# Loads of split weights written down one half tile sooner

## The chip, the core and the metric

The kernel runs on one core of a Trainium2 chip. The metric is the time of one execution on the device, in microseconds (us); smaller is better. The core has a matrix engine (TensorE, PE), three engines for elementwise work (VectorE, DVE; ScalarE, ACT; GpSimd, POOL) and SyncE (SP), whose queue starts all transfers here.

## What is computed

One layer of a hybrid decoder over 512 tokens of width 2048, in float32. The core of the reference:

```python
h = _rms(x, norm_g[l])
proj = h @ w_in[l]                              # 2048 -> 7296
pa, pb, pc = _split(proj, (A_COLS, B_COLS, C_COLS))
...
ya = _rwkv7(r, k, v, wd, ad, ...) * silu(ga)    # 12 heads of 64, a recurrence over the tokens
yb = _pool(pu, pool_w[l], pool_scale[l]) * silu(pg)
yc = _stick_breaking(qc, kc, vc, ...) * silu(gc)  # 12 heads of 64, causal
y = jnp.concatenate([ya, yb, yc], axis=-1) @ w_out[l]
x = x + y
```

## The kernel before

**Weights.** The projections are done with float32 accuracy from three products of a faster format: a weight w is split into wh (w in that format) and wl = w - wh, the input into hh and hl, and each block of 128 x 128 takes three matmuls of 512 columns, hh with wh, hl with wh, hh with wl (`three`). The unit of the stream of weights is a half tile, 128 x 1024 numbers, 512 KB: 108 of w_in (two for each tile of 128 columns of the projection behind the first three) and 32 of w_out. For each one, SP loads `raw` (2 buffers), ACT casts it to `wh` (3 buffers), DVE subtracts to `wl` (2 buffers), and PE runs 24 projection matmuls from the pair. `weights(i)` hands out half tile i and sees to it that i + 1 is written down, at high priority. In this text half tiles are counted from 1 in their order in the stream.

**The chains.** Between the projection matmuls the kernel strews the work of the three branches: six pairs of rwkv heads, six pairs of attention heads, four pooling groups. In the rwkv chain `qm`, `gm`, `gh`, `s`, `y`, `mu`, `var`, `q` and `am` are matmuls; `amr`, `bk`, `bx`, `uv`, `yc` are their operands on DVE, and `pr` and `xblk` are a long row of small DVE operations that eliminate a block of 32. In attention `z` are the scores, `n` and `w` the scans and exponentials, `wT` the transposes, `wt` their copies by ACT, `o` the products. `u` empties the projection's PSUM bank (`pj`, 2 banks).

**What sets the order.** Each branch is a generator. After every projection matmul `pump()` asks a planner, `Pace`, whether the next step of a branch may be written down: Pace keeps a clock of its own, adds up costs of matmuls, books the elementwise work of each engine (`record`) and each transfer (`transfer`, with a landing DL later by its reckoning), and a step is written down when the planner thinks that its operands are ready. The program's order so found, with the priorities of `tc.high_priority`, is the order in which every engine runs its instructions; no engine looks ahead at run time. So what the planner is told of a transfer moves the steps of the branches on all engines:

```python
def transfer(self, out, src):
    at = max(self.now, self.ready.get(self.key(src), 0.0))
    if at < self.now + 1.0:
        at = self.queue = max(at, self.queue) + 0.45
    self.ready[self.key(out)] = at + DL
```

Of the kernel before, what the change touches and what calls it, by code (L numbers as in the profile page):

```python
# [8 lines left out]
F32 = mybir.dt.float32  # L9
# [4 lines left out]
P = 128  # L14
# [41 lines left out]
AHEAD = 300  # L56
# [161 lines left out]
def hybrid_trunk_kernel(ctx: ExitStack, tc: tile.TileContext, x, xT, w_in, w_out, vecs, consts, up_w, pool_w, out):  # L218
# [5 lines left out]
    def dma(out, in_, queue=nc.sync):  # L224
        pace.transfer(out, in_)
        queue.dma_start(out=out, in_=in_)
# [3 lines left out]
    wp = ctx.enter_context(tc.tile_pool(name="wp", bufs=2))  # L230
# [9 lines left out]
    def name(s):  # L240
        uid[0] += 1
        return f"{s}_{uid[0]}"
# [199 lines left out]

    HK = KT // 2

    def split_weights(src):
        raw = wp.tile([P, HK * P], F32, tag="raw", bufs=2, name=name("raw"))
        dma(out=raw, in_=src)
        wh = wp.tile([P, HK * P], F32R, tag="wh", bufs=3, name=name("wh"))
        wl = wp.tile([P, HK * P], F32R, tag="wl", name=name("wl"))
        act.copy(out=wh, in_=raw)  # L450
        dve.tensor_tensor(wl, raw, wh.bitcast(F32), ALU.subtract)
        return wh, wl
# [9 lines left out]
    stream = []  # L462
# [7 lines left out]
    fetched = {}  # L470

    def fetch(i):
        if i < len(stream) and i not in fetched:
            with tc.high_priority(offset=AHEAD if i > 1 else 60):
                fetched[i] = split_weights(stream[i])

    def weights(i):
        fetch(i)
        fetch(i + 1)
        return fetched.pop(i)  # L480

    def project(n):
        o = pj()
        for half in range(2):
            wh, wl = weights(2 * (n - NFIRST) + half)
            for j in range(HK):
                k = half * HK + j
                sl = slice(j * P, (j + 1) * P)
                three(o, wh[:, sl], wl[:, sl], hh[k], hl[k], k == 0, k == KT - 1)
        return o  # L490
# [509 lines left out]
    for kq in range(KT // KQ):  # L1000
        parts = []
        for j in range(KQ):
            load_h(kq * KQ + j)
            if j < NFIRST:
                raw = raw0[kq, j]
# [65 lines left out]
    for nb in range(4):  # L1071
        accs = []
        for tb in range(4):
            accs.append(bank(tags[used % 8], "oacc"))
            used += 1
        for i2 in range(KT // 2):
            if nb == 0:
                split_y(2 * i2)
                split_y(2 * i2 + 1)
            wh, wl = weights(first_out + nb * (KT // 2) + i2)  # L1080
            for tb in range(4):
                ts_ = slice(tb * P, (tb + 1) * P)
                for i in (2 * i2, 2 * i2 + 1):
                    k = Y_ORDER[i]
                    sl = slice((i % 2) * 512, (i % 2) * 512 + 512)
                    three(accs[tb], yh[k][:, ts_], yl[k][:, ts_], wh[:, sl], wl[:, sl], i == 0, i == KT - 1)
        for tb in range(4):
            xr = tmp("xr")
            dma(out=xr, in_=x[tb * P:(tb + 1) * P, nb * 512:(nb + 1) * 512])
            dve.tensor_tensor(xr, accs[tb], xr, ALU.add)  # L1090
            dma(out=out[tb * P:(tb + 1) * P, nb * 512:(nb + 1) * 512], in_=xr)
# [72 lines left out]
```

## Time and profile before

| what | value |
|---|---|
| median of 3 runs | 1008.57 us (1006.39 to 1008.71) |
| the profiled execution | 1007.96 us, of which the span in the trace is 1006.1 us |
| PE busy | 978.3 us, 97% of the span |
| DVE, ACT, POOL busy | 662.2, 511.6, 140.5 us (66%, 51%, 14%) |
| mean granted clock of PE | 0.996 |
| a load of a half tile | 512 KB, 3.4 us from issue to landing |
| cast wh, subtraction wl | 1046 ns and 1246 ns, 140 of each |

A share of busy time is a mean over the span. PE's matmuls are pipelined: what counts is the distance from the start of one to the start of the next.

### The profile page before, as it was taken

To read this page: it belongs to the slowest core of one execution; us is meant where nothing else is said; L and a number is where in the kernel's file an instruction comes from. 1 tells how busy PE (TensorE), PEld (TensorE's weight loads), DVE (VectorE), ACT (ScalarE), POOL (GpSimd) and SP (SyncE) were. 2 spreads that over 40 slices of the span, in tenths; PEclk is the share of its full clock that TensorE was granted. 3 is DMA by queue.
4 is the path that set the end of the run, shared out by engine and by line. 5 is a ranking of instruction groups with operands and counts; after the bars stand their busy time and mean duration, and the time that the engine had idled before them with its cause. 6 is when DMAs were issued, how large, how long until landed. Compare 5 with 4: busy or idle time off the path is not lost. (4 is left out here: it accounts for less than half of the span.)

```text
span 1006.1 us, 13872 instructions
## 1 busy us (share of the span) xinstructions
PE 978.3 (97%) x5132; PEld 786.9 (78%) x5132; DVE 662.2 (66%) x1249; ACT 511.6 (51%) x838; POOL 140.5 (14%) x204
## 2 busy tenths in 40 slices
PE   8999999999899998999999999999999999999998
PEld 7867876888678886788768887788867888888886
DVE  5369784888849885697947979398864666323232
ACT  5656654756556654647546565466552245221210
POOL 0131211121120302112111111203211010000000
PEclk9999999999999999999999999999999999999999
DMA  9622322132321313223131222313232248624241
GB/s 337 216 90 76 103 85 90 63 111 68 105 84 58 114 65 106 79 84 95 64 121 64 90 89 80 105 63 110 72 106 79 98 145 281 219 87 147 93 138 63
DMA packets 62210, 109.17 MB, mean 109 GB/s; under 512 B 29760, under 2 KB 31168, under 8 KB 62144
## 3 DMA queue, kind: packets, MB, share of 16 engines
q1 hardware_dynamic: 62144, 108.30, 32.1%
q8 instruction: 40, 0.66, 0.3%
q14 instruction: 26, 0.21, 0.1%
HBM read 98.84 MB, written 9.44 MB: 108 GB/s over the span
## 5 line engine op out<-in xcount | busy, mean ns | idle before, releaser
L380 PE MATMUL pj<-hh,wl 128*128 128x512 f32 x864 | 343.7, 398 | 7.8 <-DVE wl L212 7.5
L380 PE MATMUL pj<-hh,wh 128*128 128x512 f32 x864 | 345.8, 400 | 0.1
L380 PE MATMUL pj<-hl,wh 128*128 128x512 f32 x864 | 343.4, 398 | 0.0
L212 DVE TENSOR_TENSOR wl<-raw,wh 128x1024 fp32r<-128x1024 f32 x140 | 174.4, 1246 | 174.6 <-PE oacc L380 86.1
L212 ACT CAST wh<-raw 128x1024 fp32r<-128x1024 f32 x140 | 146.4, 1046 | 205.7 <-PE oacc L380 95.2
L380 PEld LDWEIGHTS pj<-hh,wl 128*128 128x128 f32 x864 | 162.8, 188 | 45.7 <-DVE wl L212 12.4
L380 PEld LDWEIGHTS pj<-hh,wh 128*128 128x128 f32 x864 | 162.8, 188 | 33.6 <-issue 1.8
L380 PEld LDWEIGHTS pj<-hl,wh 128*128 128x128 f32 x864 | 163.0, 189 | 32.6 <-issue 2.2
L380 PE MATMUL oacc<-wl,yh 128*128 128x512 f32 x256 | 100.1, 391 | 0.0
L380 PE MATMUL oacc<-wh,yh 128*128 128x512 f32 x256 | 99.8, 390 | 0.0
L380 PE MATMUL oacc<-wh,yl 128*128 128x512 f32 x256 | 99.7, 390 | 0.0
L212 POOL TENSOR_SCALAR e<-e 128x512 f32<-128x512 f32 x28 | 45.2, 1614 | 197.4 <-ACT e L212 179.4
L380 PEld LDWEIGHTS oacc<-wh,yl 128*128 128x128 f32 x256 | 48.1, 188 | 10.3 <-issue 0.2
L380 PEld LDWEIGHTS oacc<-wl,yh 128*128 128x128 f32 x256 | 48.1, 188 | 10.2 <-issue 0.2
L380 PEld LDWEIGHTS oacc<-wh,yh 128*128 128x128 f32 x256 | 48.1, 188 | 10.0 <-DVE u L212 0.2
L212 POOL TENSOR_TENSOR d<-u 128x512 f32<-128x512 f32 x25 | 29.4, 1176 | 149.3 <-DVE xblk L212 67.6
L212 DVE TENSOR_TENSOR pr<-xblk,nblk 128x60 f32<-128x60 f32 (+8 forms) x180 | 46.5, 258 | 5.0
L212 ACT ACTIVATE e<-e 128x512 f32<-128x512 f32 x50 | 31.5, 630 | 35.7 <-POOL e L212 35.3
L212 DVE TENSOR_TENSOR_SCAN n<-n,m 128x512 f32<-128x512 f32 (+3 forms) x48 | 43.8, 923 | 7.5 <-ACT n L212 7.5
L212 DVE TENSOR_TENSOR xblk<-xblk,pr 128x60 f32<-128x60 f32 (+8 forms) x180 | 39.3, 218 | 5.0
L212 POOL CAST kl<-klo 64x512 fp32r<-64x512 f32 x24 | 19.2, 802 | 150.4 <-DVE klo L212 134.9
L212 ACT ACTIVATE n<-n 128x512 f32<-128x512 f32 (+1 forms) x72 | 39.6, 551 | 0.4
(203 smaller groups left out, 1227.5 us busy)
## 6 DMA issues: line engine op xcount, KB each, us to landing
raw<-in_w_in SPq DMA_DIRECT2D x108, 512.0 KB, 3.4
raw<-in_w_out SPq DMA_DIRECT2D x32, 512.0 KB, 3.4
lt<-in_x SPq DMA_DIRECT2D x8, 512.0 KB
xr<-in_x SPq DMA_DIRECT2D x16, 256.0 KB, 5.5
out<-xr SPq DMA_DIRECT2D x16, 256.0 KB, 4.1
yin<-yd SPq DMA_DIRECT2D x14, 256.0 KB, 4.6
fr<-in_w_in SPq DMA_DIRECT2D x12, 256.0 KB, 6.9
nblk<-s SPq DMA_DIRECT2D x24, 128.0 KB, 3.4
```

The lines of the kernel that those rows point to most:

```text
L212: return call(*args, **kw)
L380: pe.matmul(o, lhsT, rhs, start=start, stop=stop)
```

## The change

The load is taken out of `split_weights` into `load_weights`, and `weights(i)`, besides writing down half tile i + 1, writes down the load of half tile i + 2. The number of buffers of `raw` stays 2, and no other line changes.

```diff
--- before.py
+++ after.py
@@ -442,9 +442,16 @@
 
     HK = KT // 2
 
-    def split_weights(src):
-        raw = wp.tile([P, HK * P], F32, tag="raw", bufs=2, name=name("raw"))
-        dma(out=raw, in_=src)
+    raws = {}
+
+    def load_weights(i):
+        if i < len(stream) and i not in raws and i not in fetched:
+            raws[i] = wp.tile([P, HK * P], F32, tag="raw", bufs=2, name=name("raw"))
+            dma(out=raws[i], in_=stream[i])
+
+    def split_weights(i):
+        load_weights(i)
+        raw = raws.pop(i)
         wh = wp.tile([P, HK * P], F32R, tag="wh", bufs=3, name=name("wh"))
         wl = wp.tile([P, HK * P], F32R, tag="wl", name=name("wl"))
         act.copy(out=wh, in_=raw)
@@ -472,11 +479,13 @@
     def fetch(i):
         if i < len(stream) and i not in fetched:
             with tc.high_priority(offset=AHEAD if i > 1 else 60):
-                fetched[i] = split_weights(stream[i])
+                fetched[i] = split_weights(i)
 
     def weights(i):
         fetch(i)
         fetch(i + 1)
+        with tc.high_priority(offset=AHEAD):
+            load_weights(i + 2)
         return fetched.pop(i)
 
     def project(n):
```

Every engine has the same instructions in both kernels; their order differs. The order at two places, the first and the fourth pair of heads:

**First pair, DVE.** From the emptying of a bank by u to the emptying of the next. `u_670<-pj_561` and `u_688<-pj_563` are the same step. Before:

```order
L212 TENSOR_TENSOR u_670<-pj_561,rstd 128x512
L212 TENSOR_TENSOR wl_729<-raw_726,wh_728 128x1024
L212 TENSOR_TENSOR amr<-sq_500,E_644 64x8x64
L212 TENSOR_TENSOR c_642<-sq_500,e_619 128x512
L212 SCALAR_TENSOR_TENSOR u_559<-u_559,nvec,y_87_661 128x512
L212 SCALAR_TENSOR_TENSOR bk_693<-c_642,e_611 64x8x64
L212 SCALAR_TENSOR_TENSOR qs_570<-qm_658,qs_570 128x512
L212 TENSOR_TENSOR sl_684<-qs_681,sh_683 128x512
L212 TENSOR_TENSOR e_619<-e_619,d_485 128x512
L212 TENSOR_TENSOR wl_762<-raw_759,wh_761 128x1024
L212 TENSOR_TENSOR cq_569<-u_559,qs_570 128x512
L212 TENSOR_TENSOR bk_693<-e_619,e_611 64x8x64
```

(amr<-d,E and m stand four and five rows below the last one shown, and the next u<-pj behind m.) After:

```order
L212 TENSOR_TENSOR cq_571<-u_561,qs_572 128x512
L212 TENSOR_TENSOR wl_762<-raw_732,wh_761 128x1024
L212 TENSOR_TENSOR bk_676<-e_621,e_613 64x8x64
L212 SCALAR_TENSOR_TENSOR bk_676<-c_639,e_613 64x8x64
L212 TENSOR_TENSOR bk_676<-e_621,e_613 64x8x64
L212 TENSOR_TENSOR amr<-sq_502,E_641 64x8x64
L212 TENSOR_TENSOR amr<-d_493,E_641 128x8x64
L212 SCALAR_TENSOR_TENSOR m_90_684<-d_493,vec,e_621 128x512
L212 TENSOR_TENSOR u_688<-pj_563,rstd 128x512
L212 TENSOR_TENSOR q_124_879<-cq_571,q_124_879 64x512
L212 TENSOR_TENSOR sl_702<-qs_699,sh_701 128x512
L212 TENSOR_TENSOR u_758<-pj_690,rstd 128x512
```

The step u<-pj stood ahead of the split, and now stands behind amr<-d and m; sl has moved behind it.

**First pair, PE.** The end of one projection tile and the start of the next, at the same matmul in both. Before:

```order
L380 MATMUL pj_672<-hl_131,wh_675 128x512
L380 MATMUL pj_672<-hh_115,wl_676 128x512
L380 MATMUL pj_758<-hh_100,wh_728 128x512
L380 MATMUL pj_758<-hl_116,wh_728 128x512
L380 MATMUL pj_758<-hh_100,wl_729 128x512
L380 MATMUL pj_758<-hh_101,wh_728 128x512
L380 MATMUL qm_769<-sh_683,bmean_r 128x512
L380 MATMUL qm_769<-sl_684,bmean_r 128x512
L380 MATMUL pj_758<-hl_117,wh_728 128x512
```

After:

```order
L380 MATMUL pj_690<-hl_131,wh_691 128x512
L380 MATMUL pj_690<-hh_115,wl_692 128x512
L380 MATMUL gm_776<-amr,bk_676 128x128
L380 MATMUL gm_777<-amr,bk_676 128x128
L380 MATMUL gm_776<-amr,bk_676 128x128
L380 MATMUL pj_760<-hh_100,wh_728 128x512
L380 MATMUL pj_760<-hl_116,wh_728 128x512
L380 MATMUL pj_760<-hh_100,wl_729 128x512
L380 MATMUL pj_760<-hh_101,wh_728 128x512
```

The matmuls gm, which before stood 25 rows behind the first row shown here of tile pj_758, stand ahead of the tile now; qm stands 26 rows further down.

**Fourth pair, DVE.** The 64th and the 65th split (wl_4665 and wl_4713 before, wl_4683 and wl_4735 after) and what lies between them. Before:

```order
L212 TENSOR_TENSOR wl_4665<-raw_4662,wh_4664 128x1024
L212 TENSOR_TENSOR u_4655<-pj_4527,rstd 128x512
L212 TENSOR_TENSOR pr_4439<-xblk_4390,nblk_4389 128x28
L212 TENSOR_TENSOR xblk_4390<-xblk_4390,pr_4439 128x7x4
L212 TENSOR_TENSOR pr_4439<-xblk_4390,nblk_4389 128x21
L212 TENSOR_TENSOR xblk_4390<-xblk_4390,pr_4439 128x7x3
L212 SCALAR_TENSOR_TENSOR d_4658<-d_4658,vec,u_4655 128x512
L212 SCALAR_TENSOR_TENSOR yc_4074<-yc_4074,vec,sq_4515 128x512
L212 SCALAR_TENSOR_TENSOR n_4619<-n_4619,m_4620 128x384
L212 SCALAR_TENSOR_TENSOR yc_4074<-yc_4074,vec,bv_2960 128x512
L212 SCALAR_TENSOR_TENSOR n_4619<-n_4619,m_4620 128x128
L212 TENSOR_TENSOR y_3636<-yc_4074,y_3636 128x512
```

The next row is the 65th split. After:

```order
L212 SCALAR_TENSOR_TENSOR yc_4034<-yc_4034,vec,bv_2921 128x512
L212 TENSOR_TENSOR y_3645<-yc_4034,y_3645 128x512
L212 SCALAR_TENSOR_TENSOR n_4652<-n_4652,m_4653 128x256
L212 TENSOR_TENSOR wl_4683<-raw_4631,wh_4682 128x1024
L212 TENSOR_TENSOR u_4675<-pj_4555,rstd 128x512
L212 TENSOR_TENSOR w_4647<-w_4647,n_4652 128x256
L212 SCALAR_TENSOR_TENSOR d_4678<-d_4678,vec,u_4675 128x512
L212 TENSOR_TENSOR bv_4046<-bv_4046,d_4678 128x512
L212 TENSOR_TENSOR wl_4735<-raw_4686,wh_4734 128x1024
L212 TENSOR_TENSOR wl_4786<-raw_4738,wh_4785 128x1024
```

Of the rows that lay between the two splits, pr, xblk, yc, n and y stand ahead of the 64th now; u, d and bv are left, and a w that stood behind the 65th.

**Fourth pair, ACT.** The casts of half tiles and the copies wt (wh_4888 before and wh_4908 after are the 68th half tile's). Before:

```order
L212 CAST wh_4825<-raw_4823 128x1024
L212 COPY wt_4795<-wT_4790 128x512
L212 ACTIVATE e_4769<-d_4766 128x512
L212 ACTIVATE e_4769<-e_4769 128x512 x2
L212 CAST wh_4888<-raw_4886 128x1024
L212 COPY wt_4821<-wT_4816 128x512
L212 COPY wt_4836<-wT_4831 128x512
L212 COPY wt_4870<-wT_4867 128x256
```

After:

```order
L212 CAST wh_4855<-raw_4789 128x1024
L212 COPY wt_4802<-wT_4797 128x512
L212 ACTIVATE e_4778<-d_4775 128x512
L212 COPY wt_4811<-wT_4806 128x512
L212 ACTIVATE e_4778<-e_4778 128x512 x2
L212 CAST sh_4879<-up_4877 128x256
L212 ACTIVATE sq_4883<-d_4418,vec 128x512
L212 CAST sh_4885<-sq_4883 128x512
L212 COPY wt_4845<-wT_4842 128x256
L212 CAST wh_4908<-raw_4859 128x1024
```

The two copies wt_4821 and wt_4836 stood behind the cast of the 68th half tile; the same two, wt_4802 and wt_4811, stand ahead of it now.

## Rows read from the trace of the kernel before

**Rows 1.** The page, section 1: busy time (share of the span) and instructions of each engine.
```profile
PE 978.3 (97%) x5132; PEld 786.9 (78%) x5132; DVE 662.2 (66%) x1249; ACT 511.6 (51%) x838; POOL 140.5 (14%) x204
```

**Rows 2.** Waits of PE: who waited for whom, us in total, times, longest.
```profile
PE pj L380 <- DVE wl L212: 7.5, 8, 1.8
PE o L380 <- ACT wt L212: 4.4, 4, 1.7
PE wT L384 <- ACT w L212: 3.4, 4, 0.9
```

**Rows 3.** Timeline of PE, fourth pair: start us, us, engine, line, operation [idle before <-releaser].
```profile
470.75 0.38 PE L380 MATMUL y<-bx,uv 128*128 128x128 f32 x2
...
496.24 0.39 PE L380 MATMUL pj<-hl,wh 128*128 128x512 f32 x1
496.77 0.50 PE L380 MATMUL pj<-hh,wl 128*128 128x512 f32 x1
...
502.60 0.39 PE L380 MATMUL pj<-hl,wh 128*128 128x512 f32 x1
503.80 0.51 PE L380 MATMUL pj<-hh,wl 128*128 128x512 f32 x1 [0.80 <-DVE wl L212]
```

**Rows 4.** Windows of PE: us, PE busy (matmuls), granted clock, DMA share, GB/s.
```profile
735.30:738.70 3.40, 3.40 (x12) 0.50 0.35 135
160.00:163.50 3.50, 3.05 (x15) 1.00 0.00 0
```

**Rows 5.** Waits of SP's queue, and section 6 of the page: KB each, us to landing.
```profile
SPq L226 <- DVE wl L212: 636.4, 123, 10.7
...
raw<-in_w_in SPq DMA_DIRECT2D x108, 512.0 KB, 3.4
```

**Rows 6.** Timeline of DVE, fourth pair, with the 64th and the 65th split.
```profile
475.34 0.69 DVE L212 TENSOR_TENSOR sl<-yc,sh 128x512 fp32r<-128x512 f32 x1 [2.07 <-ACT sh L212]
...
495.50 1.22 DVE L212 TENSOR_TENSOR wl<-raw,wh 128x1024 fp32r<-128x1024 f32 x1
...
500.10 0.94 DVE L212 TENSOR_TENSOR_SCAN n<-n,m 128x384 f32<-128x384 f32 x1
...
501.61 0.41 DVE L212 TENSOR_TENSOR_SCAN n<-n,m 128x128 f32<-128x128 f32 x1
...
502.53 1.21 DVE L212 TENSOR_TENSOR wl<-raw,wh 128x1024 fp32r<-128x1024 f32 x1
```

**Rows 7.** Timeline of SP, fourth pair: loads issued.
```profile
503.81 0.33 SPq L226 DMA_DIRECT2D raw<-in_w_in  x1
...
512.02 0.39 SPq L226 DMA_DIRECT2D raw<-in_w_in  x1
```

**Rows 8.** Timeline of DVE, first pair.
```profile
78.00 0.67 DVE L212 TENSOR_TENSOR u<-pj,rstd 128x512 f32<-128x512 f32 x1
...
82.79 0.67 DVE L212 TENSOR_TENSOR sl<-qs,sh 128x512 fp32r<-128x512 f32 x1
83.39 0.67 DVE L212 TENSOR_TENSOR e<-e,d 128x512 f32<-128x512 f32 x1
...
88.94 0.75 DVE L212 SCALAR_TENSOR_TENSOR m<-d,vec,e 128x512 f32<-128x512 f32 x1
89.60 0.68 DVE L212 TENSOR_TENSOR u<-pj,rstd 128x512 f32<-128x512 f32 x1
```

**Rows 9.** Timeline of PE, first pair.
```profile
81.46 0.39 PE L380 MATMUL pj<-hh,wh 128*128 128x512 f32 x1
...
83.52 0.51 PE L380 MATMUL qm<-sl,bmean_r 128*128 128x512 f32 x1 [0.75 <-DVE sl L212]
...
89.08 1.16 PE L380 MATMUL gm<-amr,bk 64*128 64x128 f32 x16 [0.74 <-DVE amr L212]
```

**Rows 10.** Timeline of ACT, fourth pair.
```profile
473.21 1.05 ACT L212 CAST wh<-raw 128x1024 fp32r<-128x1024 f32 x1
...
515.84 1.05 ACT L212 CAST wh<-raw 128x1024 fp32r<-128x1024 f32 x1 [1.16 <-DMA raw<-in_w_in]
```

## The prediction

> **What bounds the kernel now.** I read the page first: TensorE (PE) is busy for 978.3 of 1006.1 us, VectorE (DVE) for two thirds [rows 1]. The number of matmuls doesn't change, so the change can only give or take what PE loses between them. Next I read PE's waits. From 100 us on three kinds of wait make up nearly all of its idle time: projections that wait for wl, the low half of a split weight, 7.5 us in 8 waits; attention's o that waits for the copied wt, 4.4 in 4; the transpose wT that waits for the exponential w, 3.4 in 4 [rows 2]. A wait costs some 0.16 us more than its idle time: between the starts 502.60 and 503.80 lie 1.20 us where 0.23 is usual, so 0.97 is lost with 0.80 idle [rows 3]. All of it is then 15.3 + 16 x 0.16 = 17.9 us, and some smaller waits add about 1.8 (three for wl of 0.3 each, as behind 496.24, one for s, one for mu): 19.7. The last wait for wl, 1.8 us at 732, was followed by 3.4 us at a granted clock of 0.50, its lower level of 1.2 GHz [rows 4], which cost 1.7, nearly as much again as the wait. So about **21 us** are there to be had.
>
> Why is wl late? Not because its load is. A load is 512 KB and lands after 3.4 us; the queue of loads (SP) spent 636.4 us in 123 waits for a wl [rows 5]. That is the raw buffer: there are two, and a load may only start when the split two half tiles back has read its buffer. The wl at 502.53 ends at 503.74 [rows 6], and SP issues a load at 503.81 [rows 7]. **So a load can't go a half tile sooner**: written down earlier, it waits for the same wl. The Trainium skill ("DMA: Bandwidth & Descriptors", anatomy of one DMA) says that a DMA's semaphore wait is held by the issuing sequencer, before dispatch; SP's row agrees. By that rule an early load only blocks SP's queue sooner, which speaks against the change; the third rival prices that from rows.
>
> wl is late since DVE is full. From sl at 475.34 to the split of the 64th half tile at 495.50 + 1.22 DVE has no gap of note: 21.4 us of elimination (pr, xblk), scans and splits, and PE wants that split at 496.47; the 65th, at 502.53, stands behind 5.8 us more [rows 3, 6].
>
> **The change, part by part.** The same instructions, transfers and buffers are there before and after. The raw tile is allocated a half tile sooner and the load placed on SP one to three rows earlier: nothing, as above, while a wl frees the buffer. What does change is Pace's clock: it books the load earlier, thinks wh and wl done earlier, and so places the chain steps (rwkv, attention) 20 to 40 projections sooner between the projections. The sum comes from these moves, at 0.2275 us a projection.
>
> *First pair, a loss.* In the order of before, PE had 44 projections, then qm, and gm 23 projections behind the place where gm stands now. gm needs amr, the product with E, and DVE's rows up to it are nearly the same in both. Up to 78.00 DVE has the same rows. Then u and sl have gone behind, 0.6 each by the step from 82.79 to 83.39, so amr, which ended when m began, 88.94 [rows 8], is read by gm from 89.08 on [rows 9] and now from 89.08 - 1.2 = 87.9; with ACT's squares a little later, up to 88.2. PE reaches gm at 81.46 [rows 9]. Worse, the projection behind gm needs the PSUM bank that u empties, and u now stands behind m: m begins at 88.94 - 1.2 = 87.7, and with 0.66 for m and 0.68 for u that gives 89.1, or 89.4 with ACT's delay. PE can do three gm meanwhile (0.4). It loses 89.1 - 81.46 - 0.4 = 7.2 us, or 7.5, where before qm and gm cost 0.75 and 0.74 idle [rows 9], 1.8 in all. **+5.6.** After such a gap I expect the half clock of 732 once: **+1.7**. The bounds are 0 (a gap of 1.7 us at 158 was followed by 3.5 us at full clock [rows 4]) and twice that; I take the value of the row with the longer idle stretch. The Trainium skill ("TensorE: Matmul & The Clock Gate", Part 1) has TensorE fall to its lower level after idling and climb back with work. By it this gap would surely end in half clock, as I took; without any fall the sum would be 1.7 lower.
>
> *First pair, a gain.* PE comes 5.6 us late to this pair's waits, two for wl and the longest for wt, 1.7 idle [rows 2], which are shorter than that: 3.8 of the 21 us may go.
>
> *Second pair.* The steps move by unequal amounts here. The second block of gm stands too close behind the rows that fill its operands; with DVE's pitches it waits about 1.3 us, the two gh 0.2 and 0.4, less 0.4 that goes: **+1.5**. Its two waits for wl and the one for w, 3.1 of the 21, go by the reckoning of the next part.
>
> *The steady pairs.* Take the 64th split. y, the matmul at 470.75 from which sl is made, moves 39 projections up, 8.9 us. Before, PE started it 25.7 us ahead of its need of the 64th wl; now 25.7 + 8.9 + 1.3 (two pairs of z and four transposes that come between) = 35.9 us. DVE: sl began 4.6 us after y, for ScalarE (ACT) had the cast of wh at 473.21, 1.05 us, between the two copies of yc [rows 10]. Now both copies stand together with one exponential behind: 2.4 us. Then come the 21.4 us, and 11.1 us more that used to lie outside: two splits (1.14 each), u, q and d (0.6 to 0.7 each), scans of 384 and 128 and two of 256 (0.87, 0.34, 0.60), two multiplications by w (0.94), two yc and y (1.9), and the last rows of pr and xblk (1.7). The end is at 2.4 + 21.4 + 11.1 = 34.9, **1.0 us before** the need, where it was 0.25 after. If sl takes 4.6 again, it is 1.2 late. The work between the 64th and 65th split falls from 5.8 us to 2.1 (u, w, d, bv), and PE has 24 projections, 5.5 us, between them: the wait for the 65th goes even if the 64th is late. The exponential w, which followed that split, comes with it, and wT has 31 projections, not 26, between its first two groups: those waits go too.
>
> *o.* ACT's copies of wt stood behind the cast of the 68th half tile, which began only at 515.84 [rows 10], since its load was issued only at 512.02 [rows 7], behind a transfer of lt. Now both wt stand ahead of that cast: the wait goes.
>
> Behind the second pair the gain is at most 14.2: what is left of the 21, the wait at 732 with its clock (3.6) among it. Nearer neighbours on the chain (s, gh, am) will bring small waits; I allow 0.3 a pair, **+1.5**, and count only 85% of the gains (3.8 + 3.1 + 14.2 = 21.1) since each slack is about 1 us and the reckoning no better: **-17.9**.
>
> **Sum**: 5.6 + 1.7 + 1.5 + 1.5 - 17.9 = -7.6. The profiled execution took 1007.96 us, 0.6 below the median of 1008.57, so 1000.4 beside this execution and **1001** beside the median.
>
> **Rivals.**
> 1. *Slower: DVE's full stretch stays late.* Its rows stand in a fixed order, and one late operand stops all behind it, splits too; the row of before that stood idle was sl, 2.07 us [rows 6]. If sl takes 4.6 us again and another row in the stretch waits 2.07, the 64th split is 2.2 + 2.07 - 1.0 = 3.3 us late in each of five pairs, 16 us: 1017. It decides from 1.5 us a pair, where the time is 1008.6 again. For it: the stretch is longer and gapless. Against: its operands come from steps that move up with it.
> 2. *Nothing.* The loads are held by the buffers, and what the pairs gain the first pair's hole eats: with sl 4.6 us after y, each pair loses 1.2, 6 us: 1007. For it: the first pair is nearly sure to lose, and each gain rests on about 1 us.
> 3. *SP's queue.* A load that stands sooner before the transfers of s, nblk or lt blocks them for a wait on wl, 636.4/123 = 5.2 us on the mean [rows 5]. If one of them in a pair comes that late, and 3 of the 5.2 us lie beside other work, each of five pairs loses 2: 1011. Against: in the steady order one load instead of two now stands between the first s and xblk.
> 4. *Better.* No fall of the clock, all waits gone, no small ones: 1007.96 + 5.6 + 1.5 - 21.1 = 994.
>
> **How the numbers follow.** This kernel's runs lie 2.3 us apart, so 0.3%, 3 us, is about what can be told from nothing. My forecast (995 to 1005): 0.57. Better (below 995): 0.10. Nothing (1005.5 to 1011.6): 0.16. Slower by rivals 1 and 3: 0.13 and 0.04. That gives faster 0.67, same 0.16, slower 0.17. The range, 992 to 1012, leaves out the far ends of rivals 1 and 4; the forecast's own is 995 to 1005.
>
> **What would show it.** Right: SP still waits some 600 us for wl; an idle stretch of PE from 81.5 to about 89, released by amr and then by u, with half clock behind it; no wait for wt or wT; waits for wl below 0.5 us a pair; a gm of 1 us in the second pair. Wrong: loads that SP issues away from a wl's end; a first pair whose gm meets its amr in time; five equal waits for wl of over 1 us.

## The result, and the profile after

The changed kernel takes **1018.5 us** (median of 4 runs, 1017.1 to 1019.35), the kernel before 1008.64 (4 runs); the ratio is 1.0091, with a 95% interval of 1.0066 to 1.0117. It is slower by 9 to 10 us, where I had forecast 1001. Two single executions beside the experiments, one of the kernel before at 2738.9 us and one of the kernel before with three `wl` buffers at 1072.0, were far slower than all others of their kernel and stand outside the ranges and ratios given.

The page of the profiled execution after, its first line and the busy times (us, share of the span, instructions):

```profile
span 1016.6 us, 13841 instructions
...
PE 980.3 (96%) x5132; PEld 788.4 (78%) x5132; DVE 665.6 (65%) x1249; ACT 510.3 (50%) x838; POOL 135.2 (13%) x204
```

PE is busy for 2.0 us more than before [rows 1], VectorE for 3.4 more, the others for less. So of the 10.5 us more of span 8.5 are idle time of PE. Waits of PE after (who waited for whom, us in total, times, longest):

```profile
PE pj L380 <- DVE wl L212: 11.2, 11, 2.7
PE gm L380 <- issue: 6.7, 1, 6.7
PE s L380 <- DVE bx L212: 3.8, 4, 0.9
...
PE s L380 <- DVE uv L212: 2.0, 4, 0.5
...
PE gm L380 <- DVE bx L212: 0.9, 2, 0.8
...
PE wT L384 <- issue: 0.6, 1, 0.6
PE wT L384 <- ACT w L212: 0.6, 1, 0.6
```

Beside [rows 2] the reader sees four things. The waits for wl have grown, from 7.5 us in 8 to 11.2 in 11. The waits of o for wt (4.4) are gone, those of wT are down from 3.4 to 1.2. Two kinds are new: one gap of 6.7 us ahead of gm, which the view can't put down to an engine ("issue"; the rows below show what ended it), and 5.8 us of s waiting for bx and uv in eight waits. By idle time alone that is 3.7 (wl) + 5.5 (s) + 7.1 (gm) - 4.4 (o) - 2.2 (wT) - 1.1 (qm and mu, which no longer wait), 8.6 us more than before.

The gap stands where the prediction put it. PE, first pair (start us, us, operation, [idle before]), and DVE there:

```profile
80.95 0.39 PE L380 MATMUL pj<-hh,wl 128*128 128x512 f32 x1
88.03 1.19 PE L380 MATMUL gm<-amr,bk 64*128 64x128 f32 x6 [6.70 <-issue]
89.25 0.80 PE L380 MATMUL pj<-hh,wh 128*128 128x512 f32 x1
```

```profile
87.24 0.69 DVE L212 TENSOR_TENSOR amr<-d,E 128x512 f32<-128x512 f32 x1
87.85 0.75 DVE L212 SCALAR_TENSOR_TENSOR m<-d,vec,e 128x512 f32<-128x512 f32 x1
88.51 0.68 DVE L212 TENSOR_TENSOR u<-pj,rstd 128x512 f32<-128x512 f32 x1
```

gm starts when amr<-d,E is written (87.24 + 0.69 = 87.93), the projection behind it when u has emptied its bank (88.51 + 0.68 = 89.19). What came behind, in windows of PE (us, PE busy, granted clock, DMA share, GB/s):

```profile
88.00:92.00 4.00, 3.94 (x13) 0.50 0.02 4
92.00:95.40 3.40, 3.40 (x20) 0.86 0.00 0
```

PE runs at half clock for 4 us and a part of the next 3.4 (a mean of 0.86 is 28% of it at 0.50): 4.9 us in all, which cost about 2.5.

A steady pair, the fourth, beside [rows 3, 6]. PE: the y that sl is made from, and two splits waited for, the 63rd and the 64th:

```profile
471.08 0.38 PE L380 MATMUL y<-bx,uv 128*128 128x128 f32 x2
...
502.09 0.50 PE L380 MATMUL pj<-hh,wl 128*128 128x512 f32 x1 [0.98 <-DVE wl L212]
...
509.06 0.50 PE L380 MATMUL pj<-hh,wl 128*128 128x512 f32 x1 [0.80 <-DVE wl L212]
```

DVE in the same stretch:

```profile
472.67 0.69 DVE L212 TENSOR_TENSOR w<-w,n 128x512 f32<-128x512 f32 x1
...
474.57 0.69 DVE L212 TENSOR_TENSOR sl<-yc,sh 128x512 fp32r<-128x512 f32 x1 [1.20 <-ACT sh L212]
...
475.85 0.52 DVE L212 TENSOR_TENSOR xblk<-xblk,pr 128x29 f32<-128x29 f32 x1
476.40 0.62 DVE L212 TENSOR_TENSOR pr<-xblk,nblk 128x28 f32<-128x28 f32 x1
...
481.30 0.94 DVE L212 TENSOR_TENSOR pr<-xblk,nblk 128x48 f32<-128x48 f32 x1
...
494.84 1.10 DVE L212 TENSOR_TENSOR xblk<-xblk,pr 128x54 f32<-128x54 f32 x1
...
496.25 0.74 DVE L212 SCALAR_TENSOR_TENSOR d<-d,vec,u 128x512 f32<-128x512 f32 x1
...
503.27 1.38 DVE L212 TENSOR_TENSOR_SCAN n<-n,m 128x384 f32<-128x384 f32 x2 [0.15 <-ACT n L212]
...
507.80 1.20 DVE L212 TENSOR_TENSOR wl<-raw,wh 128x1024 fp32r<-128x1024 f32 x1
```

From sl to the end of the 64th split DVE works for 507.80 + 1.20 - 474.57 = 34.4 us almost without a gap, and PE waits at both its last splits. Ahead of it ACT's exponential of w stands between the copies of yc and sh:

```profile
473.40 0.63 ACT L212 ACTIVATE w<-w 128x512 f32<-128x512 f32 x1 [0.73 <-DVE xblk L212]
```

Some 30 us sooner s waits for bx; PE, and the last bx on DVE:

```profile
442.50 0.46 PE L380 MATMUL s<-uv,bx 128*128 128x128 f32 x2 [0.94 <-DVE bx L212]
```

```profile
441.67 0.68 DVE L212 TENSOR_TENSOR bx<-gh,amr 64x512 f32<-64x512 f32 x1
```

The queue of the loads still stands behind wl, now 690.9 us in 128 waits [rows 5]:

```profile
SPq L226 <- DVE wl L212: 690.9, 128, 14.3
```

### The profile page after: what moved, and what is told of

Its sections match the earlier page's. It is cut to its first block, busy times and chain, and to the rows that moved or that the text cites. A ratio compares the mean times of both kernels' runs of the same rounds, so it can differ in the third digit from the quotient of the medians.

```text
span 1016.6 us, 13841 instructions
## 1 busy us (share of the span) xinstructions
PE 980.3 (96%) x5132; PEld 788.4 (78%) x5132; DVE 665.6 (65%) x1249; ACT 510.3 (50%) x838; POOL 135.2 (13%) x204
## 4 chain that ended last, share of the span: by engine, by line
PE 52%; DVE 21%; ACT 6%; issue 3%; POOL 1%; DMA 1%; DVEq 0%; ACTq 0%; SPq 0%; POOLq 0%
PE pj L380 26%; PE oacc L380 17%; DVE wl L212 3%; DVE bx L212 2%; DVE n L212 2%; ACT wh L212 2%; DVE pr L212 2%; DVE xblk L212 2%; PE o L380 1%; POOL e L212 1%; DMA raw<-in_w_in 1%; DVE bk L212 1%; ACT n L212 1%; DVE u L212 1%; PE wT L384 1%
## 5 line engine op out<-in xcount | busy, mean ns | idle before, releaser
L380 PE MATMUL pj<-hh,wl 128*128 128x512 f32 x864 | 344.3, 399 | 11.2 <-DVE wl L212 11.2
L212 POOL TENSOR_SCALAR e<-e 128x512 f32<-128x512 f32 x28 | 42.1, 1503 | 184.1 <-ACT e L212 183.7
L380 PEld LDWEIGHTS oacc<-wh,yl 128*128 128x128 f32 x256 | 48.0, 188 | 10.1
L212 DVE TENSOR_TENSOR_SCAN n<-n,m 128x512 f32<-128x512 f32 (+3 forms) x48 | 39.2, 827 | 20.4 <-ACT n L212 19.1
L212 DVE TENSOR_TENSOR xblk<-xblk,pr 128x60 f32<-128x60 f32 (+8 forms) x180 | 44.1, 245 | 5.0
L212 ACT ACTIVATE w<-w 128x512 f32<-128x512 f32 (+1 forms) x36 | 20.1, 559 | 43.8 <-DVE w L212 40.8
L212 POOL CAST kl<-klo 64x512 fp32r<-64x512 f32 x24 | 16.7, 695 | 181.8 <-DVE klo L212 162.2
```

The lines of the kernel that those rows point to most:

```text
L212: return call(*args, **kw)
L380: pe.matmul(o, lhsT, rhs, start=start, stop=stop)
```

## The experiments

All times are medians; ratios are to the kernel before, run beside them on the same chip (its medians there were 1009 to 1010 us).

**The place of the load against the planner's booking.** The load is written down early, but booked where it was:

```diff
-            dma(out=raws[i], in_=stream[i])
+            nc.sync.dma_start(out=raws[i], in_=stream[i])
 ...
         raw = raws.pop(i)
+        pace.transfer(raw, stream[i])
```

> The load is written down a half tile sooner, as in the change, but the planner books it where it did before. My theory (the load's place does nothing, the planner's early booking moves everything): every engine's rows stand as in the kernel before, SP's too, so 1008.6 us within 2.3. Rival (the load's place on SP's queue costs): about 1018 us, with SP's waits for wl near the 690.9 us of the change.

One run: 1010.57 us, beside runs of the kernel before of 1006.7 to 1013.2. The order of all five engines, SP's transfers too, is row by row that of the kernel before. Waits of PE, and of SP's queue:

```profile
PE pj L380 <- DVE wl L212: 7.5, 8, 1.8
```

```profile
SPq L450 <- DVE wl L212: 638.8, 123, 10.7
```

These are [rows 2, 5] again, and so are the waits of o (4.5 us) and of wT (3.4). The mirror image (booked early, written down late) gives a program in which every engine has, row by row, the order of the change; it was not run. **The place of the load in the text does nothing; the change is the planner's booking and what that moves.**

**Loads that are really free to go sooner.** The change with three raw buffers (and 14 temporary tiles for 16, which makes the room in both kernels with three):

```diff
-        raw = wp.tile([P, HK * P], F32, tag="raw", bufs=2, name=name("raw"))
+        raw = wp.tile([P, HK * P], F32, tag="raw", bufs=3, name=name("raw"))
```

> The change with three raw buffers instead of two (and 14 temporary tiles): a load written down a half tile sooner can now go sooner. Theory (no wait of the change hangs on a load; its o no longer waits): 1018 us (1016 to 1020), waits for wl within 1.5 us of 11.2. Rival (the change would have paid if the loads had been free to go): 1010 us or less.

1017.2 us, ratio 1.0075 (1.0053 to 1.0098); waits for wl 10.7 us in 10. No load is what wl waits for. The same edit on the kernel before:

> The kernel before with three raw buffers instead of two (and 14 temporary tiles instead of 16): now a load can go a half tile sooner while the order of the engines stays as before. Theory: the waits of o for wt (4.4 us idle, 5.3 lost), which hang on the late load of the 68th half tile, go; the waits for wl (7.5) don't move, since no load is what they wait for: 1004 us (1002 to 1006). Rival (loads are what wl waits for): waits for wl go too, 994 us or less. Second rival (o's wait comes back as another): 1008 us.

1004.13 us, ratio 0.9952 (0.9937 to 0.9967). Its waits of PE:

```profile
PE pj L380 <- DVE wl L212: 8.3, 9, 1.8
...
PE o L380 <- ACT wt L212: 1.7, 1, 1.7
```

o waits once instead of four times; the waits for wl stay (8.3). So the load of the 68th half tile was late for o [rows 7, 10], as the prediction had it, and a raw buffer heals that without a change of order.

**The first pair alone.** The change only from the 17th half tile on:

```diff
-            load_weights(i + 2)
+            load_weights(i + 2 if i >= 14 else -1)
```

(`load_weights` ignores -1.) The first pair then has PE's order of before, the fourth that of the change, matmul by matmul.

> The change from the 17th half tile on only: the first pair has the order of before, the steady pairs that of the change. My theory (the first pair's hole is most of the loss: PE idle 6.7 us ahead of gm and 0.4 behind, against 1.8 lost there before, and 4.5 us at half clock, 2.2): 7.5 us less than the change, 1011 us (1009.5 to 1012.5). Rival (the steady pairs' waits for wl and s are the loss): 1016 us or more.

1014.87 us, ratio 1.0046 (1.0028 to 1.0064). Against the change's 1.0091 the hole and its clock are worth some 4.5 us by the ratios and 5.4 by the two spans (1016.6 and 1011.2), not the 7.5 expected. One reason is that the first pair gets back the waits at 147 and 158, which the late PE had made 0.8 us shorter; the rest of the difference isn't accounted for. The other half of the loss, 4.6 us (2.8 to 6.5), lies behind the first pair. Of it the steady pairs have some 0.6 us each: from the first s of a pair to that of the next the change takes 118.9, 118.5 and 118.6 us, the kernel before 118.6, 117.8 and 117.8. The rest lies in the second pair and at the last wait for wl, 2.7 us where it was 1.8.

**Is wl late by its place, or because DVE is full?** Three wl buffers let a split stand up to a half tile sooner on DVE; PE's order is the same but for some 20 of 5132 places.

```diff
-        wl = wp.tile([P, HK * P], F32R, tag="wl", name=name("wl"))
+        wl = wp.tile([P, HK * P], F32R, tag="wl", bufs=3, name=name("wl"))
```

> The kernel before with three wl buffers instead of two (and 14 temporary tiles instead of 16). Theory (a split can't stand on DVE ahead of PE's end with the half tile two back, and DVE is full just then): splits stand up to a half tile sooner on DVE, all waits of PE for wl (7.5 us idle, 9.6 with restarts, 1.7 of clock) go, some of it comes back as waits for w and wt: 1000 us (997 to 1003). Rival (DVE is full and every split moved up makes the chain late by as much): 1006 to 1010 us, waits for wT, o and s longer by what wl gives.

1015.06 us, ratio 1.0048 (1.0032 to 1.0063). Waits of PE:

```profile
PE wT L384 <- ACT w L212: 13.3, 8, 2.6
```

There is no wait for wl left, but wT waits for w 13.3 us where it was 3.4. The rows of DVE and PE in the fourth pair show why:

```profile
509.57 1.21 DVE L212 TENSOR_TENSOR wl<-raw,wh 128x1024 fp32r<-128x1024 f32 x1
510.71 0.41 DVE L212 TENSOR_TENSOR w<-w,n 128x256 f32<-128x256 f32 x1
```

```profile
509.27 0.27 PE L384 MATMUL wT<-kon,w 128*128 128x128 f32 x1
511.62 0.55 PE L384 MATMUL wT<-kon,w 128*128 128x128 f32 x3 [2.07 <-ACT w L212]
```

The splits have gone ahead, and the multiplication w that wT needs stands late in the same gapless row (its exponential follows on ACT). My theory fell, and the rival's mechanism is right: what the splits win, the chain loses. Its range, 1006 to 1010 us, is missed too, by 5: the chain loses more than the splits win. With the change:

> The change with three wl buffers instead of two (and 14 temporary tiles). Theory as for the kernel before with three: the waits for wl (11.2 us idle, 13.1 with restarts) go, the hole of the first pair and the waits for s stay: 1006 us (1003 to 1009). Rival (DVE is full, the chain pays): 1015 us or more.

1024.96 us, ratio 1.0146 (1.0118 to 1.0173), waits of wT 12.4 us. The same, and worse.

**Less work for DVE.** 10 of the 30 elimination steps of each pair are left out on DVE but booked, so PE's order is unchanged (the kernel then doesn't compute the reference's output):

```diff
-            dve.tensor_tensor(prv, ...)
-            dve.tensor_tensor(xblk[:, 0:ni, j + 1:B], ...)
+            on = (dve if j % 3 else booked)
+            on.tensor_tensor(prv, ...)
+            on.tensor_tensor(xblk[:, 0:ni, j + 1:B], ...)
```

> The kernel before with the same 10 elimination steps of each pair left out, PE's order unchanged. Theory (DVE's work in that stretch is the bound): waits for wl (7.5) and for wT (3.4) nearly go, those for o (4.4, a late load) stay: 994 us (991 to 998). Rival: 1006 to 1010 us.

994.6 us (one run): as expected. Waits of PE:

```profile
PE pj L386 <- DVE wl L212: 2.5, 2, 1.3
...
PE o L386 <- ACT wt L212: 2.3, 2, 1.7
...
PE wT L390 <- ACT w L212: 1.0, 4, 0.4
```

The waits for wl fall from 7.5 to 2.5 us, those of wT from 3.4 to 1.0; those of o, which were to stay, fall from 4.4 to 2.3. In the kernel before DVE's work is the bound of that stretch. In the change:

> The change with 10 of the 30 elimination steps of each pair left out on DVE (20 of 60 small rows, about 4.4 us a pair; the output is then not the reference's), booked by the planner as before, so that PE keeps the order of the change. Theory (between y and wT each pair has more DVE work than PE gives it time, and PE pays the difference wherever the order puts it): the waits for wl (11.2 us idle, 13.1 with restarts) and the half clock behind the last go, the first pair's hole and the waits for s (5.8) stay: 1005 us (1002 to 1009). Rival (the waits come from the moved steps or from loads): 1015 us or more, waits for wl of 9 us or more.

1015.46 us, ratio 1.0065 (1.0045 to 1.0086): missed by 10. The waits for wl fall only to 7.5 us in 5. DVE in the fourth pair:

```profile
492.07 0.75 DVE L212 SCALAR_TENSOR_TENSOR d<-d,vec,u 128x512 f32<-128x512 f32 x1 [1.23 <-POOL u L212]
...
499.14 1.38 DVE L212 TENSOR_TENSOR_SCAN n<-n,m 128x384 f32<-128x384 f32 x2 [3.17 <-ACT n L212]
...
503.68 1.20 DVE L212 TENSOR_TENSOR wl<-raw,wh 128x1024 fp32r<-128x1024 f32 x1
```

The elimination is over early, and DVE stands idle for 3.17 us: in the order of the change the scans of 384 and 128 columns and four full rows stand ahead of the 64th split, and the scan waits for ACT's n. So in the change two things end at nearly the same time, DVE's work and the attention chain's operand (in the change itself the same scan, at 503.27, waited 0.15), and to take one away doesn't move the split much. That is the first rival's mechanism. (The first row shown, DVE's d, waits 1.23 us for GpSimd; the next experiment comes back to it.)

**GpSimd beside DVE.** In the change 28 of the 360 rows of pr and xblk take over 0.35 us, up to 1.1, where 0.2 is usual, 14.6 us too much in all (in the kernel before 15 rows, 10.1 us), and each of them lies beside an operation of GpSimd, 24 of 28 beside its subtraction d or its copies kl (12 of 15 before). One such pair, DVE's row at 494.84 above (1.10 us) and POOL's:

```profile
494.83 1.04 POOL L212 TENSOR_TENSOR d<-u 128x512 f32<-128x512 f32 x1 [5.87 <-DVE pr L212]
```

Here d and kl are done by ScalarE, and booked as before. d is written in another form, with the same meaning, u[t-1] mu + u[t] (1 - mu):

```diff
-        pool.tensor_tensor(d, u[:, :T], u[:, 1:], ALU.subtract)
...
+        nc.scalar.activation(d, u[:, 1:], AF.Copy, scale=omu[:, ...])
...
-        dve.scalar_tensor_tensor(s, d, mu, u[:, 1:], ALU.mult, ALU.add)
+        dve.scalar_tensor_tensor(s, u[:, :T], mu, d, ALU.mult, ALU.add)
...
-            pool.tensor_copy(out=kl2[s, :], in_=klo[s, :])
-            pool.tensor_copy(out=kl2[other, :], in_=klo[s, :])
...
+                nc.scalar.copy(out=kl2[part, :], in_=klo[s, :])
```

> The change with GpSimd's two-operand subtraction d (25 times) and its copies kl (24 times) done by ScalarE, booked by the planner as before. In the trace of the change 28 of 360 elimination rows take 0.4 to 1.1 us where 0.2 is usual, 14.6 us too much, each of them beside a GpSimd operation, mostly these two. Theory (DVE waits for GpSimd there, about 2.3 us a steady pair): long rows fall below 8, the waits for wl from 11.2 to 3 us or less: 1009 us (1006 to 1013). Rival (the long rows have another cause, or ScalarE's 28 us more make the chain late): 1016 us or more.

1007.08 us, ratio 0.9980 (0.9965 to 0.9994): 11 us less than the change. 4 long rows are left. Waits of PE:

```profile
PE gm L382 <- issue: 6.9, 1, 6.9
PE s L382 <- DVE bx L212: 3.8, 4, 0.9
...
PE wT L386 <- ACT w L212: 1.9, 2, 1.3
...
PE pj L382 <- DVE wl L212: 1.2, 3, 0.8
```

The waits for wl are down from 11.2 to 1.2; the hole and the waits for s are what is left of the change's own faults. In the fourth pair DVE's stretch from sl to the end of the 64th split is now 500.69 + 1.20 - 469.27 = 32.6 us, where the change had 34.4:

```profile
469.27 0.69 DVE L212 TENSOR_TENSOR sl<-yc,sh 128x512 fp32r<-128x512 f32 x1 [1.20 <-ACT sh L212]
...
500.69 1.20 DVE L212 TENSOR_TENSOR wl<-raw,wh 128x1024 fp32r<-128x1024 f32 x1
```

The run doesn't tell two readings apart. DVE's own d reads what GpSimd's d writes, and in the change it starts within 0.4 us of the end of GpSimd's in 11 of the 12 places where a row is long beside d (496.25 above, behind 494.83 + 1.04). Had nothing held those rows, DVE would have waited for that operand instead for most of the time, as it does at 492.07 in the run with the short elimination. So of the 14.6 us only the 4 or so beside kl are the hold's alone; of the nearly 10 beside d most would be lost to a late operand as well. Taking d off GpSimd cures both.

**Put together.** Three raw buffers, d and kl on ScalarE, on the order of before:

> The kernel before with three raw buffers and with GpSimd's d and kl done by ScalarE, booked as before. Three raw buffers alone gave 1004.1 us, with 8.3 us of waits for wl and 3.5 for wT left. Theory (DVE waits for GpSimd's d and kl in the full stretch, 10.1 us too much over 15 rows in the kernel before): waits for wl fall to 3.5 us or less, for wT to 1.5: 997 us (994 to 1000). Rival (the two gains are the same microseconds): 1003 us or more.

**993.82 us**, ratio 0.9844 (0.9827 to 0.9860): the fastest kernel of the study, and faster than expected. Waits of PE:

```profile
PE wT L386 <- ACT w L212: 3.5, 4, 1.1
...
PE o L382 <- ACT wt L212: 1.8, 2, 1.3
PE pj L382 <- DVE wl L212: 1.3, 3, 0.5
```

Waits for wl fell as expected, those for wT did not. The same two edits on the change without its first pair:

> The change from the 17th half tile on only, with three raw buffers and d and kl on ScalarE. Theory (the order of the change has two faults that DVE's fullness doesn't explain: the first pair's hole, taken out here, and about 1.75 us a pair of waits for s, which stay at 5.8 us): 1007.1 of the change with d and kl on ScalarE, less 4.5 to 7: 1001 us (999 to 1004), above the kernel before with the same two edits by 2 us or more. Rival (with DVE relieved the earlier steps pay): as fast as that kernel or faster.

996.47 us, ratio 0.9868 (0.9848 to 0.9887): faster than the 999 to 1004 expected, and 2.65 us behind the kernel before with the same edits, as expected. s is the chief wait (with 2.7 us of s for uv besides):

```profile
PE s L382 <- DVE bx L212: 3.8, 4, 1.0
```

The intervals of the two ratios overlap by a little, but each of the four runs of the one is slower than all four of the other, and from the first s of a pair to that of the next it takes 116.5 to 116.8 us against 115.3. The moved steps still win the 3.5 us of wT and 1.3 of o; the waits for s, 6.5 us where the other has 0.3, cost more.

## Why the prediction was wrong

Of the 17 us between the forecast (-7.6) and the result (+9.2 by the ratio) 16 lie behind the first pair: there the sum had 1.5 + 1.5 - 0.85 x (3.1 + 14.2) = -11.7, and the run with the change from the 17th half tile on measured +4.6.

- **Loads can't go sooner: right**, and more strictly than written. The load does not even move on SP by its place; it moves there with the chain's transfers (first experiment).
- **First pair: right in place, the loss in size too, the gain not.** I had 7.2 to 7.5 us between amr and u; PE lost 6.9 and 0.4. The clock was under-sized: 1.7 against about 2.5 us. The gain of 3.8 came only in part: the wait for wt went (1.7), but three for wl, 2.3 us idle in all, took the place of one of 1.35. Net the hole is worth 4.5 to 5.4 us; my first-pair terms, 5.6 + 1.7 - 3.8, made 3.5.
- **Steady pairs: wrong, and this is the step that failed.** I had the 64th split end 2.4 + 21.4 + 11.1 = 34.9 us after y, 1.0 us ahead of PE. It ended 507.80 + 1.20 - 471.08 = 37.9 us after y. 1.1 of the 3.0 us are sl, 3.5 us behind y and not 2.4: ACT's exponential w between yc and sh, whose cost I counted, had to wait for DVE's w, which ended at 472.67 + 0.69 = 473.36. 1.9 are the stretch itself, 34.4 for 32.5: four rows of pr and xblk beside GpSimd's kl and d (0.52, 0.62, 0.94 and 1.10) took 2.3 us more than usual, where the 21.4 us read from before held one such row, 0.9 too long. I had added the 11.1 us at usual durations and taken none for a row beside d or kl, although before has such rows. With d and kl off GpSimd the stretch measured 32.6, and no wait for wl was left in that pair, though sl was as late as in the change. So the sum of usual rows was right; what I had left out of it is GpSimd and the 1.1 us of sl. The waits came at the 63rd and the 64th split, 1.0 and 0.8 us idle, in place of the 64th and 65th, 0.3 lost and 0.8 idle [rows 3]. The 65th's wait went, as reckoned.
- **"21 us are there to be had": wrong as a premise.** I took the waits for wl, wT and wt as one stock which a better order frees. Three wl buffers show that in the order of before those for wl and wT are one debt of DVE's full stretch, which moves from one to the other (7.5 and 3.4 became 0 and 13.3). Only o's hung on a load and could be had for itself (1004.1 us). The change paid the debt at wl, for wT.
- **wT and o: right** as places (3.4 to 1.2, 4.4 to 0), and of no use, by the point above.
- **Small new waits, 1.5 us: wrong in size.** s alone waits 5.8 us idle in four pairs, 0.94 for bx and 0.5 for uv in each, and gm in the second pair 0.8. Steps moved up 20 to 40 projections while bx stayed behind a split, amr and m on DVE; I had counted the slack of before as if it moved along.
- **Rival 1** (DVE's stretch stays late, 0.13) is what happened, by its name and not by its price: some 2 us a pair and not 3.3, with sl 1.1 late and not 2.2, and no row of the stretch waiting 2.07 for an operand (the most was n, 0.15); rows beside GpSimd made up the rest. It was under-weighted since I took "its operands move up with it" as an answer; the run with the short elimination shows the operand n late by 3.2 us behind an idle DVE. Rivals 2 and 4 did not come, and rival 3 neither: SP's waits grew (636.4 to 690.9) and no wait of PE hangs on them.

What stays open: why the planner is some 6 us early for gm of the first pair alone, and whether a planner that knows of GpSimd's hold on DVE would find a better order; neither was tried. Nor was d or kl moved alone, which would part the held rows from the late operand.

## What to carry to other kernels

Where a planner or scheduler sets the order, look at what a moved line tells the planner before asking what it does on the chip: here the line itself did nothing. Before waits of one engine are added up as a stock to be had, ask whether they all fall due at the end of one stretch in which another engine has no gap; then they are that engine's debt, and more room for one of them (a third buffer) shows in one run whether the loss only moves to another. Less work for that engine is then the cure, but look for a second bound close behind: the same shorter elimination gave 14 us in one order and 3 in the other. Add durations of rows as they are in that stretch, beside whatever else runs there, and ask of a long row whether the next one would have waited anyway.

## What the runs showed of the hardware

A small DVE row (pr, xblk) that starts while GpSimd subtracts d, copies kl or masks w isn't done until that operation is: 0.2 us becomes up to 1.1. In the two kernels 70 rows start so, 29 before and 41 after, and every one of them ends 0.03 to 0.11 us behind GpSimd's end. A row that had started before GpSimd's operation keeps its 0.2 us (11 before, 19 after). The masking of w holds DVE like the other two, but it takes only 0.3 to 0.4 us as a rule, so few of its rows look long. Beside GpSimd's scaling e no such end shows in the 7 rows that start there. With d and kl gone from GpSimd, 2 to 4 rows of over 0.35 us are left; how much of the 11 us by which the kernel is faster is the hold's, no run shows. The Trainium skill ("GPSIMD Engine Reference", Specifications) says that GpSimd's way to SBUF is shared with VectorE and contended by DVE instructions with two SBUF inputs; pr and xblk are such, and the trace agrees.

The clock: a gap of 6.7 us was followed by 4.9 us at 0.50, one of 1.8 by 3.4 us, one of 1.7 by none [rows 2, 4]. With three wl buffers, where wT waits 2.1 us in each of several pairs, the mean granted clock of the whole span was 0.987 to 0.992 in nine runs, the change's 0.992 to 0.995 in four, and that of the kernel before 0.993 to 1.000.
